# First projection in order of its contraction, modulation 512 columns wide, and the other vectors' sums a step ahead, in a DiT block with a mixture of experts

## The chip, the core and the metric

The kernel runs on one core of a Trainium2 chip. The metric is the device time of one execution in microseconds (us), less is better. TensorE (PE in the profile) multiplies matrices, VectorE (DVE), ScalarE (ACT) and GpSimd (POOL) work on rows, SyncE (SP) issues most loads. Each engine runs its own list of instructions in order and waits for the others by semaphores.

## What is computed

One transformer block on x, 512 tokens of 1024 channels, with 256 context tokens, all in float32. Cut to what matters:

```python
sh1, sc1, g1, sh2, sc2, g2 = split(silu(c) @ w_ada + b_ada)          # six vectors of 1024
csh1, csc1, *_             = split(silu(c_ctx) @ w_ada + b_ada)
hc = rms_norm(ctx, norm_mix) * (1 + csc1) + csh1
hx = rms_norm(x,   norm_mix) * (1 + sc1)  + sh1
q, zf_f, zf_b, i, g, gate_b, gate_c, v = split(hx @ w_in)            # eight sections of 512 columns
s_f, s_b = context_states(hc @ w_in[:, 512:2048])                    # zf_f, zf_b and i of ctx
o = gated_linear_attention(q, i, zf_f, zf_b, s_f, s_b)               # four heads, two directions
y = gate_b * conv3(gate_c * v)
x = x + g1 * (concat(rms_norm(o) * silu(g), y) @ w_out)
h2 = rms_norm(x, norm_ffn) * (1 + sc2) + sh2
x = x + g2 * expert_choice_ffn(h2)                                   # 16 experts, 64 tokens each
out = rms_norm(x, norm_final)
```

## The kernel before

All activations are kept transposed: channels on the 128 partitions, tokens in the free dimension. A weight of `w_in` or of the normalised input is split into a high and a low part in TensorE's fast float32 format (`whi`, `wlo`, L257 and L258; `h_hi`, `h_lo`, L292 to L294), and each product of the projections is made of three (L265, L266, L270 for x, L268, L269, L272 for ctx); `products` runs over the eight blocks `k` of the contraction for one block of 128 output columns at a time.

**Start.** SP loads ctx and the two halves of x (`xt`, L91), then weights in tiles of 1 MB (`stream`). `rms_rows` (L217, L220) normalises rows, `transpose_ctx` (L228) and `transpose_x` (L237) turn them on TensorE.

**Modulation.** The first two vectors, scale and shift, are worked out 256 columns at a time in eight units: `ada_unit` (L187) makes eight products, each with 32 columns of the array (`k % 4` chooses which 32), ACT copies the sum (L190), `ada_cols` transposes it twice (L197) and DVE adds the four groups (L198, L201). After each pair of units the two blocks `k` that it serves are modulated (L292 to L294), and section 1 (`zf_f`) uses them: its first half of 256 columns is made for two `k` at a time with four accumulators (`first`, two of x and two of ctx), its second half by `project_T` after all units.

**The other four vectors** (gate 1, shift 2, scale 2, gate 2) aren't made on TensorE: `ada_sum` loads 128x8x256 of `w_ada` and adds eight scaled tiles on DVE (L533, L535); one product with ones then adds over the partitions, as rows (`ada_r`, L543, with a DVE add L544) or as columns (`ada_c`, L550). `more_ada(j)` does one row sum and two column sums; it stands after the second half of section 1, the halves of section 2 and section 4. The four row sums of gate 2 (`g2b`) stand among the sections 6, 7, 5 in the head stage (`sections`).

**Then** come section 3 (`project_i`, L335) with the context states (`context_state`, L373 to L390), whose temporaries lie in the pool `p_c`; the router weight `wr`, loaded by POOL's queue (L613) behind `g2b` (L610) into the pool `rowb`, which takes the memory of the pools just released, and multiplied on DVE (L615); the head stage, which mixes attention of the four heads with the products of sections 0, 6, 7 and 5; the output projection, the router, and the experts (L897, L855, L954, L929), most of the time.

A scheduler sets the order on each engine: instructions are placed by the order of the program and by priority (`tc.high_priority`), each when its inputs can be there. In the code names have an index that the rows leave out.

Of the kernel before, what the change touches and what calls it, by code (L numbers as in the profile page):

```python
# [38 lines left out]
def dit_block(ctx, tc, x, c, ctx_in, c_ctx, w_ada, b_ada, norm_mix, norm_ffn, w_in, lb_logits,  # L39
# [164 lines left out]
    def ada_scale(ev, col0, dst, gain):  # L204

        ada_cols(ev, col0, dst)
        dve.tensor_scalar(dst, dst, 1.0, None, op0=ALU.add)
        dve.tensor_tensor(dst, dst, gain.unsqueeze(2).to_broadcast([P, 2, 2]), op=ALU.mult)
# [67 lines left out]
    first = None
    for j in range(4):
        ksl = slice(2 * j, 2 * j + 2)
        wsc, wsh = (stream(wa_r[:, :, at:at + 256], f"wa_{at}") for at in (D + 256 * j, 256 * j))
        with tc.high_priority(offset=PRIO if j else 0):  # L280
            ada_scale(ada_unit(D + 256 * j, wsc), D + 256 * j, a1[:, ksl], col("nmix", 2 * j, 2))
            ada_cols(ada_unit(256 * j, wsh), 256 * j, b1[:, ksl])
# [784 lines left out]
```

## Time and profile before

| | us |
|---|---|
| median of 3 runs | 1338.11 (1332.74 to 1338.48) |
| the profiled execution | 1336.76 |
| its span, first to last instruction | 1334.8 |
| TensorE busy | 1264.9 (95%) |
| DVE busy | 420.5 (32%) |
| ACT busy | 245.0 (18%) |
| POOL busy | 43.6 (3%) |
| data moved | 458.85 MB, mean 344 GB/s |

The profile is of one execution. PE is TensorE's products, PEld its weight loads, which overlap them. A float32 product leaves two records, one in the split format leaves one. PEclk is the granted TensorE clock as a share of full speed. In a row of the timeline the first number is the start, the second the duration, and the bracket at the end the idle time ahead of it and what ended that.

### The profile page before, as it was taken

How to read it: one execution, taken by the hardware profiler on the slowest of the kernel's cores; microseconds unless marked ns; L12 is line 12 of the kernel's file. 1: busy time of each engine (PE TensorE's matmuls, PEld its weight loads, DVE VectorE, ACT ScalarE, POOL GpSimd, SP SyncE). 2: the span in 40 equal slices, each digit the busy share in tenths (PEclk: the TensorE clock that was granted, in tenths of full speed). 3: DMA queues.
4: the chain of work that ended last, by engine and by line, in shares of the span. 5: the costliest groups of instructions: out<-in, count | busy, mean ns of one | idle time of the engine just before them, and what ended most of it. 6: DMA issues, size and time to landing. Idle time of an engine off the chain costs nothing.

```text
span 1334.8 us, 15459 instructions
## 1 busy us (share of the span) xinstructions
PE 1264.9 (95%) x6374; PEld 692.5 (52%) x6374; DVE 420.5 (32%) x969; ACT 245.0 (18%) x494; POOL 43.6 (3%) x51
## 2 busy tenths in 40 slices
PE   5999989998969999999999999999999999999996
PEld 3788978776844443444444344344434434443433
DVE  5776467986451112112101211211021121102114
ACT  5633444334211200010000001000000100000002
POOL 1000022140000000000000000000000000000000
PEclk9999989998979999999999999999999999999998
DMA  9868223316389989999999999999999999999996
GB/s 328 267 201 261 96 82 96 127 64 234 143 330 407 358 347 426 426 427 427 427 426 426 425 427 427 427 427 426 425 427 427 427 427 426 427 425 427 426 385 215
DMA packets 112082, 458.85 MB, mean 344 GB/s; under 512 B 7310, under 2 KB 56571, under 8 KB 64907
## 3 DMA queue, kind: packets, MB, share of 16 engines
q1 hardware_dynamic: 110832, 454.06, 84.6%
q0 software_dynamic: 992, 3.74, 0.8%
q8 instruction: 50, 0.82, 0.2%
q14 instruction: 22, 0.17, 0.0%
q10 hardware_dynamic: 186, 0.06, 0.0%
HBM read 455.73 MB, written 2.10 MB: 343 GB/s over the span
## 4 chain that ended last, share of the span: by engine, by line
PE 87%; DVE 7%; ACT 3%; DMA 2%; issue 1%; POOL 0%; DVEq 0%; ACTq 0%; POOLq 0%; SPq 0%
PE gu L897 37%; PE y L954 17%; PE pg L855 5%; PE po L929 3%; PE px L265 3%; PE px L266 3%; PE px L270 3%; PE ht L912 2%; PE y L1009 1%; PE wo L710 1%; PE wo L711 1%; PE wo L712 1%; DMA wd<-in_w_down 1%; PE pi L335 1%; PE pi L333 1%
## 5 line engine op out<-in xcount | busy, mean ns | idle before, releaser
L897 PE MATMUL gu<-wg,xs 128*64 128x512 f32 x1024 | 461.7, 599 | 0.7 <-ACT gs L907 0.7
L897 PE MATMUL gu<-wu,xs 128*64 128x512 f32 x1024 | 460.7, 599 | 0.0
L954 PE MATMUL y<-wd,hid 128*64 128x512 f32 x896 | 239.2, 598 | 0.0
L897 PEld LDWEIGHTS gu<-wg,xs 128*64 128x64 f32 x1024 | 128.7, 136 | 158.1 <-issue 154.3
L897 PEld LDWEIGHTS gu<-wu,xs 128*64 128x64 f32 x1024 | 128.7, 136 | 123.1 <-issue 122.5
L907 DVE COPY gs<-gu 128x512 f32<-128x512 f32 x32 | 22.0, 691 | 389.8 <-PE gu L897 389.8
L954 PEld LDWEIGHTS y<-wd,hid 128*64 128x64 f32 x896 | 82.2, 136 | 120.1 <-issue 113.8
L907 ACT COPY gs<-gu 128x512 f32<-128x512 f32 x32 | 18.7, 587 | 455.1 <-PE gu L897 455.1
L265 PE MATMUL px<-h_hi,whi 128*128 128x512 f32 x208 | 85.1, 409 | 0.0
L270 PE MATMUL px<-h_hi,wlo 128*128 128x512 f32 x208 | 84.0, 404 | 0.0
L855 PEld LDWEIGHTS pg<-ohr,x 128*128 128x128 f32 x512 | 62.4, 195 | 40.6 <-issue 38.9
L266 PE MATMUL px<-h_lo,whi 128*128 128x512 f32 x208 | 83.4, 401 | 0.0
L855 PE MATMUL pg<-ohr,x 128*128 128x128 f32 x512 | 71.8, 289 | 1.5 <-DVE ohr L847 1.5
L861 DVE TENSOR_SCALAR xs<-pg,a,b 128x128 f32<-128x128 f32 x32 | 13.1, 410 | 149.1 <-PE pg L855 149.1
L258 DVE TENSOR_TENSOR wlo<-wi,whi 128x1024 fp32r<-128x1024 f32 x32 | 42.3, 1326 | 34.4 <-ACT whi L257 34.3
L923 DVE SCALAR_TENSOR_TENSOR yt<-y,gate,g2b 128x512 f32<-128x512 f32 (+1 forms) x17 | 12.2, 719 | 128.8 <-PE y L954 108.6
L535 DVE SCALAR_TENSOR_TENSOR adas<-wa,cs,adas 128x256 f32<-128x256 f32 x112 | 51.5, 492 | 1.2
L858 ACT ACTIVATE xs<-pg,b,a 128x128 f32<-128x128 f32 x32 | 14.6, 457 | 199.7 <-PE pg L855 199.7
L929 PE MATMUL po<-yhl,g 128*128 128x512 f32 (+1 forms) x136 | 41.7, 418 | 7.5 <-ACT yhl L924 7.0
L265 PEld LDWEIGHTS px<-h_hi,whi 128*128 128x128 f32 x208 | 40.2, 193 | 8.4 <-issue 0.4
L966 DVE TENSOR_TENSOR acc<-acc,po 128x512 f32<-128x512 f32 x56 | 36.0, 684 | 26.8 <-PE po L929 26.8
L929 PEld LDWEIGHTS po<-yhl,g 128*128 128x128 f32 x136 | 22.4, 189 | 42.1 <-ACT yhl L924 14.3
(323 smaller groups left out, 1310.2 us busy)
## 6 DMA issues: line engine op xcount, KB each, us to landing
wg<-in_w_gate SPq DMA_DIRECT2D x128, 1024.0 KB, 17.4
wu<-in_w_up SPq DMA_DIRECT2D x128, 1024.0 KB, 18.1
wd<-in_w_down SPq DMA_DIRECT2D x124, 1024.0 KB, 19.5
wa<-in_w_ada SPq DMA_DIRECT2D x22, 1024.0 KB, 7.0
wi<-in_w_in SPq DMA_DIRECT2D x16, 1024.0 KB, 5.4
wo<-in_w_out SPq DMA_DIRECT2D x4, 1024.0 KB, 5.2
wd<-in_w_down SPq DMA_DIRECT2D x16, 256.0 KB, 5.9
xt<-in_x SPq DMA_DIRECT2D x2, 1024.0 KB, 7.7
```

The costliest lines, as they stand in the source:

```text
L258: dve.tensor_tensor(lo, v, hi.bitcast(F32), op=ALU.subtract)
L265: mm(px, hi[:, k], h_hi[:, k], start=f, stop=False)
L266: mm(px, hi[:, k], h_lo[:, k], start=False, stop=False)
L270: mm(px, lo[:, k], h_hi[:, k], start=False, stop=l)
L535: dve.scalar_tensor_tensor(acc, t[:, k * 256:(k + 1) * 256], cs[:, k, 0:1], acc, op0=ALU.mult, op1=ALU.add)
L855: mm(pg[:, :P], x1[:, tb, k * P:(k + 1) * P], ohr[:, tb], start=tb == 0, stop=tb == NT - 1)
L897: mm(gu[n][i * CAP:(i + 1) * CAP], xs[:, k, ssl], w[:, n * 512:(n + 1) * 512], start=k == 0, stop=k == KD - 1, skip_group_check=True)
L907: (act.copy if n % 2 else dve.tensor_copy)(to, fr)
L912: pe.transpose(pt[:, i * P:(i + 1) * P], gs[:, f * P:(f + 1) * P], ident)
L929: mm(po, g[:, tb * P:(tb + 1) * P], yhl[:, i, nsl], start=first and i == 0, stop=i == 1)
L954: mm(y[n][i * CAP:(i + 1) * CAP], hid[:, i, f], wd[i][:, s, n * 512:(n + 1) * 512], start=f == 0, stop=f == DFF // P - 1, skip_group_check ...
L966: dve.tensor_tensor(acc[tb][:, nsl], acc[tb][:, nsl], po, op=ALU.add)
```

## The change

Section 1 is made in the order of its contraction. `w_in` comes in two tiles of 512 rows by 512 columns; after the first pair of units, blocks 0 to 3 of x are multiplied with all 512 output columns (four accumulators of x, `first_x`), then blocks 0 to 3 of ctx (two banks, `first_c`), then blocks 4 to 7 of both. X is loaded, normalised and transposed first; ctx is loaded behind the first weights, and its rows are normalised and transposed behind the first products of x, through the bank "tp".

The modulation has four units of 512 columns instead of eight of 256. Their two tiles have rows of 2 KB instead of 1 KB. The transposes and the DVE reduction become four products with `sel`, a matrix of 128x2 that adds the groups.

The other vectors have eight sums of 512 columns instead of sixteen of 256, and the generator `others` makes the product of a sum one step after the sum: a step is one block of section 2, a half of section 4, or a half of section 3. Those of gate 2 lie there too, none in the head stage. `g2b` is loaded at the start. The gate's `kk` (L365 before) is issued after the table load that the projections are followed by. All else is as before.

```diff
-    for src, name in ((cx_r, "xt_c"), (x_r[:, 0:2], "xt_0"), (x_r[:, 2:4], "xt_1")):
+    for src, name in ((x_r[:, 0:2], "xt_0"), (x_r[:, 2:4], "xt_1"), (cx_r, "xt_c")):
         t = early.tile([P, 2048], F32, name=name)
-        sp.dma_start(out=t.rearrange("p (a b) -> p a b", a=2), in_=src)
+        if name != "xt_c":
+            sp.dma_start(out=t.rearrange("p (a b) -> p a b", a=2), in_=src)
         xt.append(t)
+    xt = xt[2:] + xt[:2]
...
+    def ada_loads(col0):
+        return [stream(wa_r[:, 4 * q:4 * q + 4, col0:col0 + 512], f"wa_{col0}_{q}")
+                for q in range(2)]
+
+    def ada_unit(col0, ts):
+        pa = bank("o", 1, f"ada_{col0}")
         for k in range(KD):
             g = k % 4
-            mm(pa[32 * g:32 * g + 32, :256], cs[:, k, :], t[:, k * 256:(k + 1) * 256],
+            mm(pa[32 * g:32 * g + 32], cs[:, k, :], ts[k // 4][:, g * 512:(g + 1) * 512],
                start=k < 4, stop=k >= 4, skip_group_check=True)
-        ev = early.tile([P, 256], F32, tag="adaev", name=f"ada_ev_{col0}", bufs=2)
-        act.copy(ev, pa[:, :256])
+        ev = early.tile([P, 512], F32, tag="adaev", name=f"ada_ev_{col0}", bufs=1)
+        act.copy(ev, pa)
         return ev
...
+    def ada_cols(ev, col0, dst, bias):
 
         pt = bank("tp", 1, f"ada_t_{col0}")
-        for b in range(2):
-            pe.transpose(pt[:, b * P:(b + 1) * P], ev[:, b * P:(b + 1) * P], ident)
-        dve.tensor_reduce(dst, pt[:, :256].rearrange("p (b g m) -> p b m g", b=2, g=4)[:, :, 0:2],
-                          op=ALU.add, axis=AX.X)
-        o = off["b_ada"] + col0 // P
-        dve.tensor_tensor(dst, dst, cols[:, o:o + 2].unsqueeze(2).to_broadcast([P, 2, 2]),
-                          op=ALU.add)
+        for b in range(4):
+            mm(pt[:, 2 * b:2 * b + 2], ev[:, b * P:(b + 1) * P], sel, start=b == 0, stop=b == 3,
+               skip_group_check=True)
+        dve.tensor_tensor(dst, pt[:, 0:8].rearrange("p (b m) -> p b m", b=4),
+                          bias.unsqueeze(2).to_broadcast([P, 4, 2]), op=ALU.add)
+
+    def ada_shift(ev, j, dst):
+        ada_cols(ev, 512 * j, dst, col("b_ada", 4 * j, 4))
+
+    def ada_scale(ev, j, dst, gain):
+
+        ada_cols(ev, D + 512 * j, dst, bias1[:, 4 * j:4 * j + 4])
...
-            pt = bank("mm", 4, f"pt_c_{k2}")
+            pt = bank("tp", 1, f"pt_c_{k2}")
...
+    first_x = [bank("mm", 4, f"px_f{i}") for i in range(4)]
+    first_c = [bank(tag, 1, f"pc_f_{tag}") for tag in ("sc", "kv")]
+    first_w = {}
...
+    def first_products(k, ctx_too):
+        hi, lo = (t[:, k % 2] for t in first_w[k // 2])
+        for i in range(4):
+            f, l, bs = k == 0, k == KD - 1, slice(i * P, (i + 1) * P)
+            if ctx_too:
+                pc = first_c[i // 2][:, (i % 2) * CTX:(i % 2 + 1) * CTX]
+                mm(pc, hi[:, bs], hc_hi[:, k], start=f and i % 2 == 0, stop=False,
+                   skip_group_check=True)
+                mm(pc, hi[:, bs], hc_lo[:, k], start=False, stop=False, skip_group_check=True)
+                mm(pc, lo[:, bs], hc_hi[:, k], start=False, stop=l, skip_group_check=True)
+            else:
+                mm(first_x[i], hi[:, bs], h_hi[:, k], start=f, stop=False)
+                mm(first_x[i], hi[:, bs], h_lo[:, k], start=False, stop=False)
+                mm(first_x[i], lo[:, bs], h_hi[:, k], start=False, stop=l)
+
+    def first_parts(n):
+        hi, lo = (p_h.tile([P, 2, 512], F32R, tag="whl", name=f"w{q}_1_{n}", bufs=6)
+                  for q in ("hi", "lo"))
+        v = raws[n // 2].rearrange("p (k n) -> p k n", k=4)[:, 2 * (n % 2):2 * (n % 2) + 2]
+        act.copy(hi, v)
+        dve.tensor_tensor(lo, v, hi.bitcast(F32), op=ALU.subtract)
+        first_w[n] = hi, lo
...
+    def modulation(j):
+        ksl = slice(4 * j, 4 * j + 4)
+        ada_scale(ada_unit(D + 512 * j, wsc[j]), j, a1[:, ksl], col("nmix", 4 * j, 4))
+        ada_shift(ada_unit(512 * j, wsh[j]), j, b1[:, ksl])
+
+    wsc, wsh = [ada_loads(D)], [ada_loads(0)]
+    first_raw = lambda i: stream(wi_r[:, 4 * i:4 * i + 4, 512:1024], f"wi_1_{i}")
+    raws = [first_raw(0)]
+    sp.dma_start(out=xt[0].rearrange("p (a b) -> p a b", a=2), in_=cx_r)
+    for i in range(2):
+        rms_rows(xt[1 + i], f"x{i}")
+    with tc.high_priority(offset=PRIO):
+        modulation(0)
+    transpose_x()
+    wsc.append(ada_loads(D + 512))
+    wsh.append(ada_loads(512))
+    raws.append(first_raw(1))
+    for j in range(2):
+        ks = range(4 * j, 4 * j + 4)
+        for n in (2 * j, 2 * j + 1):
+            first_parts(n)
+            for k in (2 * n, 2 * n + 1):
+                modulate(xnT, h_hi, h_lo, k, 0)
+        for k in ks:
+            first_products(k, False)
         if j == 0:
             rms_rows(xt[0], "c")
             transpose_ctx()
-            for i in range(2):
-                rms_rows(xt[1 + i], f"x{i}")
-            transpose_x()
-        for k in (2 * j, 2 * j + 1):
-            for src, hi, lo, m in ((xnT, h_hi, h_lo, 0), (cnT, hc_hi, hc_lo, 1)):
-                sca, sft = a1[:, k, m:m + 1], b1[:, k, m:m + 1]
-                act.activation(hi[:, k], src[:, k], AF.Identity, scale=sca, bias=sft)
-                dve.tensor_scalar(src[:, k], src[:, k], sca, sft, op0=ALU.mult, op1=ALU.add)
-                dve.tensor_tensor(lo[:, k], src[:, k], hi[:, k].bitcast(F32), op=ALU.subtract)
-        if first is None:
-            parts = split_w(1, 0)
-            first = [(bank("mm", 4, f"px_f{i}"), bank("mm", 4, f"pc_f{i}")) + parts[i]
-                     for i in range(2)]
-        for px, pc, hi, lo in first:
-            products(px, pc, hi, lo, (2 * j, 2 * j + 1))
+        for k in ks:
+            modulate(cnT, hc_hi, hc_lo, k, 1)
+            first_products(k, True)
+        if j == 0:
+            with tc.high_priority(offset=80):
+                modulation(1)
...
+        with tc.issue_after(tables.ins):
+            act.activation(kk, s, AF.Identity, scale=noml[:, i:i + 1], bias=oml[:, i:i + 1])
...
-        t = stream(wa_r[:, :, col0:col0 + 256], f"wa_{col0}")
-        acc = p_sig.tile([P, 256], F32, tag="adas", name=f"adas_{col0}", bufs=2)
-        dve.tensor_scalar(acc, t[:, :256], cs[:, 0, 0:1], None, op0=ALU.mult)
+        ts = ada_loads(col0)
+        acc = p_c.tile([P, 512], F32, tag="adas", name=f"adas_{col0}", bufs=2)
+        dve.tensor_scalar(acc, ts[0][:, :512], cs[:, 0, 0:1], None, op0=ALU.mult)
         for k in range(1, KD):
-            dve.scalar_tensor_tensor(acc, t[:, k * 256:(k + 1) * 256], cs[:, k, 0:1], acc,
-                                     op0=ALU.mult, op1=ALU.add)
+            dve.scalar_tensor_tensor(acc, ts[k // 4][:, (k % 4) * 512:(k % 4 + 1) * 512],
+                                     cs[:, k, 0:1], acc, op0=ALU.mult, op1=ALU.add)
...
+    g2b = const.tile([P, D], F32, name="g2b")
+    tc.keep_in_program_order(gp.dma_start(out=g2b, in_=bass.AP(
+        tensor=b_ada.tensor, offset=b_ada.offset + 5 * D, ap=[[0, P], [1, D]])))
...
+    def others():
+
+        last = None
+        for i, dst in ((3, b2), (4, a2), (2, g1b), (5, g2b)):
+            for j in range(2):
+                col0 = i * D + 512 * j
+                acc = ada_sum(col0)
+                if last:
+                    last()
+                if i == 3:
+                    last = lambda a=acc, c=col0, j=j: more_cols(a, c, b2[:, 4 * j:4 * j + 4])
+                elif i == 4:
+                    last = lambda a=acc, c=col0, j=j: more_scale(a, c, a2[:, 4 * j:4 * j + 4],
+                                                                 col("nffn", 4 * j, 4))
+                else:
+                    last = lambda a=acc, c=col0, j=j, d=dst: more_rows(a, c, d[:, 512 * j:512 * j + 512])
+                yield
+        last()
+        yield
+
+    more = others()
+    keep = keep_sig(0)
+    for i in range(4):
+        keep[0](i, first_x[i])
+        keep[1](i, first_c[i // 2][:, (i % 2) * CTX:(i % 2 + 1) * CTX])
+    for half in range(2):
+        for _ in project_T(2, half, *keep_sig(1)):
+            next(more)
     for half in range(2):
         run(project_T(4, half, keep_g))
-    more_ada(3)
-    tc.keep_in_program_order(act.preload_act_table_set("natural_log_exp_and_others"))
+        next(more)
...
+    tables = tc.keep_in_program_order(act.preload_act_table_set("natural_log_exp_and_others"))
     for half in range(2):
         project_i(half)
+        next(more)
         for h in (2 * half, 2 * half + 1):
             for d in range(2):
                 context_state(d, h)
+    run(more)
     p_c.release()
...
-    g2b = rowb.tile([P, D], F32, name="g2b")
-    gp.dma_start(out=g2b, in_=bass.AP(tensor=b_ada.tensor, offset=b_ada.offset + 5 * D,
-                                      ap=[[0, P], [1, D]]))
...
-                if i < 2:
-                    at = 256 * (2 * half + i)
-                    more_rows(5 * D + at, g2b[:, at:at + 256])
```

On TensorE, in section 1, behind the first products of x. `ada` are the units' sums (`spare` and `wa` their weights), `pt_c` transposes of ctx, `pc_f` products of ctx, `px_f` of x. Before:

```order
L270 MATMUL px_f_328<-h_hi,wlo_0_1_323 128x512
L187 MATMUL ada_504<-wa_500,cs 32x256 x8
L272 MATMUL pc_f_329<-hc_hi,wlo_0_1_323 128x256
L265 MATMUL px_f_326<-h_hi,whi_0_0_318 128x512
L268 MATMUL pc_f_327<-hc_hi,whi_0_0_318 128x256
```

Now:

```order
L311 MATMUL px_f_158<-h_hi,wlo_1_302 128x512
L193 MATMUL ada_457<-spare,cs 32x512
L239 MATMUL pt_c_373<-ident,xt_c 128x128
L193 MATMUL ada_457<-spare,cs 32x512
L239 MATMUL pt_c_373<-ident,xt_c 128x128
...
L304 MATMUL pc_f_sc<-hc_hi,whi_0_291 128x256
L304 MATMUL pc_f_kv<-hc_hi,whi_0_291 128x256
L306 MATMUL pc_f_sc<-hc_lo,whi_0_291 128x256
L307 MATMUL pc_f_sc<-hc_hi,wlo_0_292 128x256
L193 MATMUL ada_475<-wa_0_285,cs 32x512
L239 MATMUL pt_c_385<-ident,xt_c 128x128 x4
L193 MATMUL ada_475<-wa_0_285,cs 32x512 x3
L193 MATMUL ada_475<-wa_1_287,cs 32x512
L239 MATMUL pt_c_391<-ident,xt_c 128x128 x4
L193 MATMUL ada_475<-wa_1_287,cs 32x512 x3
```

A unit's eight products stood in one piece; now those of the first take turns with single transposes, eight times, and those of the second stand in three pieces.

On DVE, around the router weight's multiply (`wr`). `kk_c`, `pr_c`, `sigc` belong to context states, `wlo` to the splits of the next section. Before:

```order
L258 TENSOR_TENSOR wlo_1_0_1881<-wi_1_1878,whi_1_0_1880 128x1024
L373 SCALAR_TENSOR_TENSOR pr_c_1702<-ones,sigc_3_711 128x256
L379 TENSOR_TENSOR kk_c_1699<-kk_c_1699,sigc_3_711 128x256
L615 TENSOR_TENSOR wr_1761<-wr,a_585 128x128
L373 SCALAR_TENSOR_TENSOR pr_c_1719<-ones,sigc_3_1039 128x256
L377 TENSOR_TENSOR sigc_3_1039<-pr_c_1719,sigc_3_1039 128x256
```

Now:

```order
L598 TENSOR_TENSOR g2b<-g2b,ada_r_1556 128x512
L269 TENSOR_TENSOR wlo_1_0_1777<-wi_1_1774,whi_1_0_1776 128x1024
L428 SCALAR_TENSOR_TENSOR pr_c_1597<-ones,sigc_3_649 128x256
L598 TENSOR_TENSOR g2b<-g2b,ada_r_1629 128x512
L682 TENSOR_TENSOR wr_1657<-wr,a_633 128x128
L434 TENSOR_TENSOR kk_c_1594<-kk_c_1594,sigc_3_649 128x256
L428 SCALAR_TENSOR_TENSOR pr_c_1614<-ones,sigc_3_936 128x256
L432 TENSOR_TENSOR sigc_3_936<-pr_c_1614,sigc_3_936 128x256
```

The multiply stood behind the second to last context state's `kk`; now it stands ahead of it, and two adds of gate 2 stand close before.

On DVE in the head stage, at the norm of a head (`om`, `ou`, `or`, `on`). Before:

```order
L489 TENSOR_SCALAR om_2114<-os_2113 128x4
L426 TENSOR_TENSOR q2d_1755<-qT_1854,ex_2146 128x4x4x32
L490 TENSOR_TENSOR ou_2116<-or_2115 128x4
L533 TENSOR_SCALAR adas_2680<-wa_2678,cs 128x256
L491 TENSOR_TENSOR ou_2116<-ou_2116,om_2114 128x4
L535 SCALAR_TENSOR_TENSOR adas_2680<-wa_2678,cs,adas_2680 128x256
L492 TENSOR_SCALAR ou_2116<-ou_2116 128x4
L535 SCALAR_TENSOR_TENSOR adas_2680<-wa_2678,cs,adas_2680 128x256
```

Now:

```order
L544 TENSOR_SCALAR om_2010<-os_2009 128x4
L473 TENSOR_TENSOR kk_2030<-ki_2045,dte_2037 128x512
L545 TENSOR_TENSOR ou_2012<-or_2011 128x4
L546 TENSOR_TENSOR ou_2012<-ou_2012,om_2010 128x4
L547 TENSOR_SCALAR ou_2012<-ou_2012 128x4
L548 TENSOR_TENSOR or_2011<-or_2011,ou_2012 128x4
```

The sums of gate 2 (`adas`) stood between the steps of the norm; none is left there.

## Rows read from the trace of the kernel before

**Rows 1.** The page, chain that ended last, by engine.

```profile
PE 87%; DVE 7%; ACT 3%; DMA 2%; issue 1%; POOL 0%; DVEq 0%; ACTq 0%; POOLq 0%; SPq 0%
```

**Rows 2.** Busy time by stretch; columns as in the first line here.

```profile
core 0: us, PE busy (x) PEld busy (x) DVE busy (x) ACT busy (x) POOL busy (x), PEclk, DMA share, GB/s
0.00:26.50 26.50, 12.01 (x85) 8.76 (x85) 12.72 (x52) 14.05 (x26) 3.98 (x13) 1.00 0.98 323
...
71.40:131.70 60.30, 60.30 (x327) 51.90 (x325) 44.50 (x102) 20.13 (x28) 0.00 (x0) 1.00 0.72 226
...
170.90:206.00 35.10, 31.12 (x135) 25.51 (x134) 21.99 (x43) 14.29 (x30) 12.23 (x12) 0.85 0.38 117
206.00:311.00 105.00, 101.24 (x744) 83.81 (x742) 87.79 (x162) 40.31 (x93) 24.58 (x21) 0.98 0.28 90
...
390.50:1295.00 904.50, 890.81 (x3978) 387.59 (x3978) 141.65 (x322) 76.30 (x155) 0.54 (x1) 1.00 1.00 417
```

**Rows 3.** Timeline of PE, 12 to 33 us.

```profile
24.01 1.97 PE L237 MATMUL pt_x<-ident,xt 128*128 128x128 f32 x16 [0.17 <-ACT xnT L240]
26.56 0.49 PE L265 MATMUL px_f<-h_hi,whi 128*128 128x512 f32 x1 [0.58 <-ACT whi L257]
...
31.78 1.07 PE L187 MATMUL ada<-spare,cs 128*32 128x256 f32 x16
```

**Rows 4.** Timeline of DVE, then of ACT, 12 to 30 us.

```profile
15.50 1.42 DVE L220 TENSOR_SCALAR xt<-xt,r1r 128x1024 f32<-128x1024 f32 x2
...
21.18 0.75 DVE L220 TENSOR_SCALAR xt<-xt,r1r 128x1024 f32<-128x1024 f32 x1
...
24.75 0.81 ACT L292 ACTIVATE h_hi<-xnT,b,a 128x512 fp32r<-128x512 f32 x1 [0.31 <-DVE b L201]
25.47 1.03 ACT L257 CAST whi<-wi 128x1024 fp32r<-128x1024 f32 x1
```

**Rows 5.** Timeline of PE, 60 to 74 us.

```profile
61.94 0.39 PE L265 MATMUL px<-h_hi,whi 128*128 128x512 f32 x1
62.17 0.40 PE L266 MATMUL px<-h_lo,whi 128*128 128x512 f32 x1
62.40 0.28 PE L268 MATMUL pc<-hc_hi,whi 128*128 128x256 f32 x1
62.52 0.27 PE L269 MATMUL pc<-hc_lo,whi 128*128 128x256 f32 x1
...
71.41 0.59 PE L543 MATMUL ada_r<-adas,ones 128*128 128x256 f32 x2
71.84 0.50 PE L550 MATMUL ada_c<-ones,adas 128*128 128x2 f32 x4
72.21 0.48 PE L265 MATMUL px<-h_hi,whi 128*128 128x512 f32 x1
```

**Rows 6.** Timeline of all engines, 168 to 184 us.

```profile
170.88 0.55 POOL L610 DMA_DIRECT2D g2b<-in_b_ada  x1 [150.85 <-PE pt_c L382]
171.42 0.92 POOL L613 DMA_DIRECT2D wr<-in_w_router  x1
...
178.78 0.29 DVE L615 TENSOR_TENSOR wr<-wr,a 128x128 f32<-128x128 f32 x1 [4.04 <-DMA wr<-in_w_router]
...
181.19 0.41 PE L382 MATMUL pt_c<-ident,kk_c 128*128 128x128 f32 x2 [3.98 <-DVE kk_c L379]
```

**Rows 7.** Busy time and clock, two stretches after idle time; columns as in rows 2.

```profile
182.80:193.10 10.30, 10.30 (x36) 8.82 (x35) 7.53 (x17) 5.60 (x11) 5.36 (x5) 0.53 0.33 104
...
244.20:247.70 3.50, 3.50 (x10) 2.73 (x10) 3.50 (x9) 0.00 (x0) 0.00 (x0) 0.58 0.02 5
```

**Rows 8.** Waits of PE, 206 to 311 us: total, times, longest.

```profile
PE kv L456 <- ACT kT L443: 2.6, 2, 2.1
```

**Rows 9.** Groups of DVE, 206 to 311 us: busy, mean ns, idle before.

```profile
L535 DVE SCALAR_TENSOR_TENSOR adas<-wa,cs,adas 128x256 f32<-128x256 f32 x14 | 8.0, 572 | 0.1
...
L544 DVE TENSOR_TENSOR g2b<-g2b,ada_r 128x256 f32<-128x256 f32 x4 | 1.6, 412 | 0.0
```

More of the change, by code (lines that the diff above doesn't have):

```diff
@@ L204, in ada_scale @@
[L204 to L208, printed above, removed]
+        ev = early.tile([P, 512], F32, tag="adaev", name=f"ada_ev_{col0}", bufs=1)
+        act.copy(ev, pa)
+        return ev
+    sel = const.tile([P, 2], F32, name="sel")
+    dve.tensor_reduce(sel, ident.rearrange("p (g m) -> p m g", g=4)[:, 0:2], op=ALU.add, axis=AX.X)
@@ new lines, in dit_block @@
+    bias1 = const.tile([P, 8], F32, name="bias1")
+    dve.tensor_scalar(bias1, col("b_ada", 8, 8), 1.0, None, op0=ALU.add)
+    def ada_cols(ev, col0, dst, bias):
+        pt = bank("tp", 1, f"ada_t_{col0}")
+        for b in range(4):
[3 more added lines that the diff above has]
+                          bias.unsqueeze(2).to_broadcast([P, 4, 2]), op=ALU.add)
@@ L211, in dit_block @@
+    def ada_shift(ev, j, dst):
+        ada_cols(ev, 512 * j, dst, col("b_ada", 4 * j, 4))
+    def ada_scale(ev, j, dst, gain):
+        ada_cols(ev, D + 512 * j, dst, bias1[:, 4 * j:4 * j + 4])
+        dve.tensor_tensor(dst, dst, gain.unsqueeze(2).to_broadcast([P, 4, 2]), op=ALU.mult)
     xnT = early.tile([P, KD, SEQ], F32, tag="xnT", name="xnT")
@@ L275, in dit_block @@
     b1 = const.tile([P, KD, 2], F32, name="b1")
[L276 to L282, printed above, removed]
+    first_x = [bank("mm", 4, f"px_f{i}") for i in range(4)]
@@ new lines, in dit_block, with modulate @@
+    first_c = [bank(tag, 1, f"pc_f_{tag}") for tag in ("sc", "kv")]
+    first_w = {}
+    def modulate(src, hi, lo, k, m):
+        sca, sft = a1[:, k, m:m + 1], b1[:, k, m:m + 1]
+        act.activation(hi[:, k], src[:, k], AF.Identity, scale=sca, bias=sft)
+        dve.tensor_scalar(src[:, k], src[:, k], sca, sft, op0=ALU.mult, op1=ALU.add)
+        dve.tensor_tensor(lo[:, k], src[:, k], hi[:, k].bitcast(F32), op=ALU.subtract)
+    def first_products(k, ctx_too):
[12 more added lines that the diff above has]
+                mm(first_x[i], lo[:, bs], h_hi[:, k], start=False, stop=l)
@@ L364, in gates @@
         kk = pool.tile([P, w], F32, tag="kk", name=f"kk_{nm}", bufs=2)
-        act.activation(kk, s, AF.Identity, scale=noml[:, i:i + 1], bias=oml[:, i:i + 1])
+        with tc.issue_after(tables.ins):
+            act.activation(kk, s, AF.Identity, scale=noml[:, i:i + 1], bias=oml[:, i:i + 1])
         act.activation(s, s, AF.Ln, scale=oml[:, i:i + 1], bias=lb[:, i:i + 1])
@@ L510, in keep_gc @@
     def keep_gc(i, px):
-        cv[i] = p_sig.tile([P, SEQ], F32, tag="cv", name=f"cv_{i}", bufs=2)
+        cv[i] = p_in.tile([P, SEQ], F32, tag="cv", name=f"cv_{i}", bufs=2)
         act.copy(cv[i], px)
@@ L537, in ada_sum, with more_rows @@
-        return acc
-    def more_rows(col0, dst):
-        acc = ada_sum(col0)
+            dve.scalar_tensor_tensor(acc, ts[k // 4][:, (k % 4) * 512:(k % 4 + 1) * 512],
+                                     cs[:, k, 0:1], acc, op0=ALU.mult, op1=ALU.add)
+        return acc
+    def more_rows(acc, col0, dst):
         pg = bank("mm", 4, f"ada_r_{col0}")
-        mm(pg[:, :256], ones[:, :P], acc, start=True, stop=True)
-        dve.tensor_tensor(dst, dst, pg[:, :256], op=ALU.add)
-    def more_cols(col0, dst):
-        acc = ada_sum(col0)
+        mm(pg, ones[:, :P], acc, start=True, stop=True)
+        dve.tensor_tensor(dst, dst, pg, op=ALU.add)
@@ L548, in more_cols @@
+    def more_cols(acc, col0, dst):
         pg = bank("tp", 1, f"ada_c_{col0}")
-        for b in range(2):
+        for b in range(4):
             mm(pg[:, 2 * b:2 * b + 2], acc[:, b * P:(b + 1) * P], ones[:, 0:2], start=b == 0,
-               stop=b == 1, skip_group_check=True)
+               stop=b == 3, skip_group_check=True)
         o = off["b_ada"] + col0 // P
-        dve.tensor_tensor(dst, pg[:, 0:4].rearrange("p (b m) -> p b m", b=2),
-                          cols[:, o:o + 2].unsqueeze(2).to_broadcast([P, 2, 2]), op=ALU.add)
@@ L556, in more_scale @@
-    def more_scale(col0, dst, gain):
-        more_cols(col0, dst)
+        dve.tensor_tensor(dst, pg[:, 0:8].rearrange("p (b m) -> p b m", b=4),
+                          cols[:, o:o + 4].unsqueeze(2).to_broadcast([P, 4, 2]), op=ALU.add)
+    def more_scale(acc, col0, dst, gain):
+        more_cols(acc, col0, dst)
         dve.tensor_scalar(dst, dst, 1.0, None, op0=ALU.add)
-        dve.tensor_tensor(dst, dst, gain.unsqueeze(2).to_broadcast([P, 2, 2]), op=ALU.mult)
+        dve.tensor_tensor(dst, dst, gain.unsqueeze(2).to_broadcast([P, 4, 2]), op=ALU.mult)
@@ L572, in dit_block @@
-    for d in range(2):
-        for half in range(2):
-            keep = keep_sig(d)
-            if d == half == 0:
-                for i, (px, pc, hi, lo) in enumerate(first):
-                    keep[0](i, px)
-                    keep[1](i, pc[:, :CTX])
-            else:
-                run(project_T(1 + d, half, *keep))
-                more_ada(2 * d + half - 1)
+    def others():
[16 more added lines that the diff above has]
+        yield
```

8 lines of the change are left out of this document (removed).

## Prediction, written before the changed kernel was run

> **What bounds the kernel now.** I read the chain of waits first: TensorE holds 87% of it, DVE 7%, DMA 2% [rows 1]. Whatever shortens TensorE's own list of work, or its idle time, moves the end. Then the stages, by a table of stretches: in the longest one, the experts, TensorE is busy 890.81 of 904.50 us [rows 2]. The change touches nothing there, and the loads of that part start when buffers of the head stage come free, so it shifts as a whole by what the first 311 us gain or lose. Those early stages differ. In the projections of 71 to 132 us TensorE never rests, while DVE works 44.50 of 60.30 us: there work moved onto DVE is free, work on TensorE is paid in full. Around the router weight, 171 to 206 us, and in the head stage, 206 to 311 us, TensorE idles 35.10 - 31.12 = 4.0 and 105.00 - 101.24 = 3.8 us [rows 2]: only there can a wait be won.
>
> The sum is made against the profiled execution, 1336.76 us, 1.35 below the median of 1338.11 and inside the runs' 1332.74 to 1338.48. A measurement can tell some 0.5%, 6.7 us, from no change.
>
> **Start of the products.** Before, the last tile of x is normalised at 21.18 + 0.75 = 21.9 us, behind ctx and the first x tile (ready at 15.50 + 1.42 = 16.9) [rows 4], and the first product starts at 26.56 [rows 3]. Now x comes first, so its last tile should be ready when its first one was, at 16.9. After it stand, in the order listed: 8 transposes (half of the 1.97 for 16 [rows 3], 1.0); the second half of the scale unit; 16 more transposes (2.0); its sums by `sel`; the shift unit; its eviction and sums; two modulations and one split.
>
> What a unit costs: 8 products of 256 columns on 32 array columns each take 1.07 us together [rows 3]. One float32 product of 256 columns costs 71.84 - 71.41 = 0.43 us [rows 5], so four column groups do run at once (two rounds, 0.86) and 0.21 goes into the change of shape. At 512 columns two rounds are 1.72, a packed unit 1.93, half of one 1.0. The sums by `sel` are 4 products with two columns; two such products, in four records, took 72.21 - 71.84 = 0.37 [rows 5], so 0.74. Eviction of 512 columns: no more than the 0.81 of the activation of that shape [rows 4]. So 16.9 + 1.0 + 1.0 + 2.0 + 0.74 + 1.93 + 0.8 + 0.74 + 2 x 0.81 + 1.03 [rows 4] = 27.8, and one wait like the 0.58 ahead of the first product now [rows 3]: **28.4**. What x won, the wider units take back.
>
> **The first section.** It ends at 71.41 now [rows 5]. After: 28.4, plus 96 products of x at 62.17 - 61.94 = 0.23 us (22.1) and 96 of ctx at 62.52 - 62.40 = 0.12 (11.5) [rows 5], plus three things now behind the first product: 16 ctx transposes (2.0; they ran while TensorE had nothing else to do), two sums by `sel` (1.5), and the other two units. These are the doubtful ones. The order puts products of the first of them singly between ctx transposes of full width, and cuts the second into three pieces. Then the groups can't run together: a product alone is 2 x 0.43 = 0.86 and, by the 0.21 found above, 1.07 with its change of shape; 8 x 1.07 + 3 x 1.07 = 11.8. No row shows such an alternation. [...] The end is 28.4 + 22.1 + 11.5 + 2.0 + 1.5 + 11.8 = 77.3: **+5.9**.
>
> [...] The row of the unit shows 0.21 us beyond two rounds of streams [rows 3]. [...]
>
> Ctx is loaded eighth now. Eight loads of 1.05 MB at the 323 GB/s of the first 26.5 us [rows 2] are in by 26 us, and its normalising has to begin by about 33, six us ahead of its transposes; I count no wait.
>
> **Sections two to four.** Before, these held four row sums (0.43) and eight column sums (0.37) [rows 5]: 4.7 us. Now four column sums of twice the width (0.74) and one row sum (0.86): 3.8. **-0.9.** DVE's part, now with 512 columns in an operation, hides in the 16 us that DVE has free there [rows 2]; the sum being a step ahead, TensorE doesn't wait for it. Table loads that go are on ACT and hide behind products: nothing. The third 512-wide row sum and its DVE add go into the projection of i: +0.86, with 0.37 of column sums less, and some 1 us for context states that now have fewer products between them: **+1.5** (0 to 2.5).
>
> **The router weight.** POOL issues g2b at 170.88 and the router weight behind it at 171.42; DVE's multiply waits 4.04 us for it, the context state behind that on DVE waits too, and TensorE idles 3.98 until 181.19 [rows 6]. The idle engine then runs 10.30 us at a clock of 0.53 [rows 7], a loss of some (1 - 0.53) x 10.30 = 4.8. Together 8.8. Now g2b is loaded at the start, const; the router weight still waits for the same memory to come free and its flight remains (178.78 less 171.42 is 7.4 us [rows 6], which it had to share). On DVE its multiply stands ahead of one more context state, so less work is left to cover the flight; against that, two row sums of 0.86 (+1.7) fill TensorE. I take 2.0 us of idle time and half of the slow clock, 2.4: 1.7 + 2.0 + 2.4 = 6.1 instead of 8.8: **-2.7**. Bounds: nothing but the 1.7 is left (-7.1), or the wait stays and 1.7 is added (+1.7).
>
> **The head stage.** Four row sums leave it: 4 x 0.43 = 1.7 on TensorE. On DVE 8.0 us of multiplies and 1.6 of adds go [rows 9], and they stand among the steps whose results TensorE and ACT wait for. Its idle 3.8 us there is for keys from ACT, 2.6 of it [rows 8], that come behind DVE's steps, and the clock after it, 0.58 for 3.50 us, costs 1.5 [rows 7]. I give the change 80% of 5.3: 4.3. **-6.0**, bounds -1.7 and -7.0.
>
> Sum: +5.9 - 0.9 + 1.5 - 2.7 - 6.0 = -2.2, from 1336.76: **1334.6 us**.
>
> **The rivals.** *The alternation costs nothing.* The column groups overlap across the transposes; for it, that they do so inside a unit [rows 3]. 11.8 becomes 3.9: 1334.6 - 7.9 = 1326.7. Against it: TensorE takes its list in order, and each transpose needs all columns. Chance 0.12.
>
> *The router weight comes early.* With the queue to itself it lands before it is asked for; stall and slow clock vanish. 4.4 better, 1330.2. For it, that it was issued only 0.54 us behind the other load [rows 6] and landed with it; against it, the longer queue on DVE. Chance 0.17.
>
> [...] Chance 0.11.
>
> *DVE doesn't hold the head stage.* The wait for keys is ACT's own, as the row names ACT [rows 8]; then only the 1.7 of TensorE is won, 4.3 worse: 1338.9. Chance 0.09.
>
> **How the numbers follow.** The forecast has 0.51. Its own terms (1.5 on the projection of i, 4 on the router weight, 2 on the head stage) give 1330 to 1339. The range, 1325 to 1345, takes in the first, second and fourth rivals with their edges and stops just short of the third's price; outside lie the third rival and a few edges, under 0.2. Faster than 1331.4: the first rival, two thirds of the second, a tenth of the forecast: 0.12 + 0.11 + 0.05 = 0.28. Slower than 1344.8: the third, and 0.02 where the upper ends of several terms meet: 0.13. The rest 0.59.
>
> **What would show it.** In the trace after: first product near 28.4; narrow products and transposes in turn near 39 to 49 at about 1.07 a pair; the first section's end near 77.3; from there to the projection of i one us less than before; around the router weight an idle time of about 2 us in place of 3.98 and a clock above 0.53; the head stage about 99 us instead of 105, with less than 1 us waited for keys; and the experts' 904.5 unchanged. The prediction is wrong if the units take 4 us, if the clock drops there, or if the experts' stage itself changes in length.

## The result, and the profile after

The change is slower: 1346.07 us (1345.24 to 1347.96, four runs) against 1335.55 (1332.74 to 1338.48), a ratio of 1.0095 with an interval of 1.0071 to 1.0118. The forecast was 1334.6, range 1325 to 1345. The profiled execution took 1345.24 us, its span is 1343.5, 8.7 longer than before. The loads in the page's 40 slices tell something at once, before:

```profile
GB/s 328 267 201 261 96 82 96 127 64 234 143 330 407 358 347 426 426 427 427 427 426 426 425 427 427 427 427 426 425 427 427 427 427 426 427 425 427 426 385 215
```

and now:

```profile
GB/s 359 196 198 254 204 104 68 63 64 286 137 327 394 356 363 422 421 421 420 421 421 421 421 421 420 421 421 421 421 421 421 420 422 421 421 421 421 421 371 229
```

From slice 16 to 38 it was 425 to 427 GB/s, and now it is 420 to 422.

The stretches of the changed kernel, cut where its stages end (columns as in [rows 2]):

```profile
core 0: us, PE busy (x) PEld busy (x) DVE busy (x) ACT busy (x) POOL busy (x), PEclk, DMA share, GB/s
0.00:28.50 28.50, 12.51 (x82) 7.32 (x82) 11.79 (x47) 11.88 (x21) 2.64 (x11) 0.99 0.94 354
28.50:42.40 13.90, 13.90 (x48) 10.97 (x48) 7.32 (x15) 4.50 (x7) 1.88 (x3) 0.78 0.90 336
42.40:57.00 14.60, 14.60 (x54) 3.99 (x53) 3.17 (x8) 5.34 (x10) 0.00 (x0) 1.00 0.27 75
57.00:80.90 23.90, 23.86 (x160) 21.60 (x158) 19.78 (x35) 13.13 (x20) 0.00 (x0) 1.00 0.55 184
80.90:140.10 59.20, 59.20 (x324) 51.13 (x323) 37.24 (x55) 14.25 (x23) 0.00 (x0) 1.00 0.76 254
...
176.00:213.00 37.00, 34.07 (x212) 27.78 (x211) 23.61 (x40) 18.79 (x35) 12.37 (x11) 1.00 0.29 85
213.00:311.00 98.00, 95.05 (x695) 79.36 (x693) 80.21 (x142) 40.16 (x91) 24.64 (x21) 1.00 0.23 77
```

The clock is 1.00 around the router weight (176 to 213), where it was 0.53 for 10.30 us [rows 7], and in the alternating stretch (42.4 to 57); it is low (0.78) where before it wasn't, behind 28.5 us. TensorE's timeline shows the first section:

```profile
24.70 1.05 PE L208 MATMUL ada_t<-sel,ada_ev 128*128 128x2 f32 x8 [0.76 <-ACT ada_ev L196]
28.50 0.79 PE L309 MATMUL px_f<-h_hi,whi 128*128 128x512 f32 x1 [2.74 <-ACT whi L317]
29.09 0.63 PE L310 MATMUL px_f<-h_lo,whi 128*128 128x512 f32 x1
...
42.46 1.04 PE L193 MATMUL ada<-spare,cs 128*32 128x512 f32 x2
43.43 0.33 PE L239 MATMUL pt_c<-ident,xt_c 128*128 128x128 f32 x1
43.69 1.04 PE L193 MATMUL ada<-spare,cs 128*32 128x512 f32 x2
...
52.17 0.36 PE L304 MATMUL pc_f_sc<-hc_hi,whi 128*128 128x256 f32 x1
...
54.40 1.07 PE L193 MATMUL ada<-wa,cs 128*32 128x512 f32 x8
...
80.89 0.39 PE L276 MATMUL px<-h_hi,whi 128*128 128x512 f32 x1
```

The first product starts at 28.50 (26.56 before [rows 3]). A product of a unit in turn with a transpose takes 43.69 - 42.46 = 1.23 us a pair; four products in one piece take 1.07 together (eight records, two to a product). Section 2 starts at 80.89.

Around the router weight, all engines (answers to [rows 6]):

```profile
179.79 0.92 POOL L680 DMA_DIRECT2D wr<-in_w_router  x1 [144.19 <-PE pi L389]
...
180.14 1.02 PE L597 MATMUL ada_r<-adas,ones 128*128 128x512 f32 x2
...
185.92 0.29 DVE L682 TENSOR_TENSOR wr<-wr,a 128x128 f32<-128x128 f32 x1 [2.75 <-DMA wr<-in_w_router]
...
186.69 0.41 PE L437 MATMUL pt_c<-ident,kk_c 128*128 128x128 f32 x2 [2.93 <-DVE kk_c L434]
```

TensorE idles 2.93 us instead of 3.98. In the head stage the waits of TensorE are now these (190 to 311 us); the wait for `kT`, 2.6 us [rows 8], is gone:

```profile
PE sc L502 <- POOL q2d L486: 0.5, 1, 0.5
PE pt_o L557 <- DVE on L550: 0.3, 1, 0.3
PE o L531 <- DVE both L528: 0.2, 1, 0.2
```

So the first section ends later than before (80.89 us for 71.41), and the stages behind it win that back: the output projection's first product starts at 315.11 us, where before it started at 317.07, 2.0 us ahead. What makes the change slower lies behind that, in the experts. The gathers of each second expert (`pg`) mark the pace there. Before:

```profile
930.90 1.38 PE L855 MATMUL pg<-ohr,x 128*128 128x128 f32 x10
...
1046.61 1.38 PE L855 MATMUL pg<-ohr,x 128*128 128x128 f32 x10
...
1162.31 1.38 PE L855 MATMUL pg<-ohr,x 128*128 128x128 f32 x10
```

After:

```profile
929.59 1.38 PE L919 MATMUL pg<-ohr,x 128*128 128x128 f32 x10
...
1050.18 1.38 PE L919 MATMUL pg<-ohr,x 128*128 128x128 f32 x10
...
1169.45 1.38 PE L919 MATMUL pg<-ohr,x 128*128 128x128 f32 x10
```

At 930 us the changed kernel is still 1.3 us ahead. Up to there a pair of experts takes 115.71 us in both. Then it takes 120.59 and 119.27 in the changed one. By the last product the 1.3 us ahead have become 8.7 behind (1332.5 us for 1323.8).

A pair of experts loads 48 tiles of 1.05 MB, 50.3 MB; in 115.71 us that is 435 GB/s, more than the loads give in either kernel. So the loads fall behind TensorE all the time, and TensorE lives on the buffers that were filled ahead. At 427 GB/s a pair is short by 115.71 x (1 - 427/435) = 2.1 us, at 421 by 3.7 (estimates from these rows). The spacings fit: at 427 the reserve lasts to the end, at 421 to a point behind 930 us, and after that a pair takes 119.27 us, which is 50.3 MB at 422 GB/s, the rate of the loads. What has to be explained is the 421.

### The profile page after: what moved, and what is told of

Read it like the earlier page. It is cut to its first block, busy times and chain, and to the rows that moved or that the text cites. A ratio compares the mean times of both kernels' runs of the same rounds, so it can differ in the third digit from the quotient of the medians.

```text
span 1343.5 us, 15244 instructions
## 1 busy us (share of the span) xinstructions
PE 1276.5 (95%) x6318; PEld 690.5 (51%) x6318; DVE 409.5 (30%) x877; ACT 237.3 (18%) x484; POOL 44.3 (3%) x51
## 4 chain that ended last, share of the span: by engine, by line
PE 91%; DVE 4%; DMA 2%; ACT 2%; issue 1%; POOL 0%; DVEq 0%; SPq 0%; POOLq 0%; ACTq 0%
PE gu L961 38%; PE y L1018 17%; PE pg L919 5%; PE px L276 3%; PE px L277 3%; PE px L281 3%; PE po L993 3%; PE ht L976 2%; PE y L1073 1%; PE wo L774 1%; PE ada L193 1%; PE wo L775 1%; PE wo L776 1%; DMA wd<-in_w_down 1%; PE pi L389 1%
## 5 line engine op out<-in xcount | busy, mean ns | idle before, releaser
L961 PE MATMUL gu<-wg,xs 128*64 128x512 f32 x1024 | 462.4, 599 | 0.7 <-ACT gs L971 0.7
L276 PE MATMUL px<-h_hi,whi 128*128 128x512 f32 x192 | 76.8, 400 | 0.0
L281 PE MATMUL px<-h_hi,wlo 128*128 128x512 f32 x192 | 75.3, 392 | 0.0
L277 PE MATMUL px<-h_lo,whi 128*128 128x512 f32 x192 | 74.9, 390 | 0.0
L269 DVE TENSOR_TENSOR wlo<-wi,whi 128x1024 fp32r<-128x1024 f32 x28 | 37.4, 1335 | 27.3 <-ACT whi L268 27.2
L590 DVE SCALAR_TENSOR_TENSOR adas<-wa,cs,adas 128x512 f32<-128x512 f32 x56 | 41.4, 748 | 1.4 <-DMA wa<-in_w_ada 0.4
L976 PE MATMUL ht<-ident,gs 128*128 128x128 f32 x256 | 34.9, 279 | 6.9 <-DVE hid L980 6.9
```

The source lines that it names most:

```text
L269: dve.tensor_tensor(lo, v, hi.bitcast(F32), op=ALU.subtract)
L276: mm(px, hi[:, k], h_hi[:, k], start=f, stop=False)
L277: mm(px, hi[:, k], h_lo[:, k], start=False, stop=False)
L281: mm(px, lo[:, k], h_hi[:, k], start=False, stop=l)
L590: dve.scalar_tensor_tensor(acc, ts[k // 4][:, (k % 4) * 512:(k % 4 + 1) * 512], cs[:, k, 0:1], acc, op0=ALU.mult, op1=ALU.add)
L961: mm(gu[n][i * CAP:(i + 1) * CAP], xs[:, k, ssl], w[:, n * 512:(n + 1) * 512], start=k == 0, stop=k == KD - 1, skip_group_check=True)
```

## The experiments

**Theory A:** the address of the weight buffers. In the built program the twelve weight buffers of `ring_b` start at byte 80896 of a partition before, a multiple of 512; in the changed one at 80960, 64 further. `g2b` left `rowb` for `const`, both ahead of `ring_b`, which cancels; `sel` and `bias1`, of 8 and 32 bytes, take the 64. The four buffers of `ring_a` lie 352 and 416 bytes past a multiple of 512. **Theory B:** the order of the work, or the state in which the stage is entered.

The first six kernels (a_b0 to a_ra0_b64 below) differ from their base in unused tiles alone; every engine's list of instructions is the same as in the base. The unused tile in `rowb` moves what is allocated behind it on the same side by the same bytes: the twelve buffers, and some tiles that hold no streamed weights (the router's, the parts of `w_out`, the rows that the experts gather).

**a_b0**, changed kernel:

```diff
     rowb = tc.alloc_tile_pool(name="rowb", bufs=1, side="left")
+    rowb.tile([P, 112], F32, name="pad")
```

> The changed kernel with an unused tile of 448 bytes per partition in the pool rowb, which lies ahead of the twelve weight buffers of the experts (ring_b); every engine's list of instructions stays as it is, and the buffers start at a multiple of 512 bytes again, as before the change, instead of 64 bytes past one. Theory A, the address of the buffers sets the rate of the loads: loads of the experts' stage back at 427 GB/s instead of 421, pairs of experts 115.7 us apart to the end instead of 119.3 in the last third, and the time is what the first 315 us say, 2 us under the kernel before: about 1334. Theory B, the order of the work or the state in which the stage is entered slows the loads: 421 GB/s and 1346 as the change.

Measured: 1334.85 us, ratio to before 1.0002 (0.9988 to 1.0016; each ratio is against runs of the kernel before that were taken beside it, with medians of 1332.45 to 1334.62). Its stretches in the experts:

```profile
550.00:950.00 400.00, 394.64 (x1767) 172.69 (x1764) 61.04 (x136) 31.26 (x66) 0.00 (x0) 1.00 1.01 427
950.00:1250.00 300.00, 295.63 (x1310) 127.19 (x1309) 48.86 (x104) 23.11 (x48) 0.54 (x1) 1.00 1.01 426
```

and those of the change:

```profile
550.00:950.00 400.00, 394.65 (x1767) 172.75 (x1764) 61.07 (x136) 31.31 (x66) 0.00 (x0) 1.00 1.01 421
950.00:1250.00 300.00, 295.63 (x1268) 126.39 (x1265) 48.19 (x102) 22.56 (x47) 0.54 (x1) 1.00 1.01 421
```

The loss shows in a count only: from 950 on, 1268 records of products against 1310 in 300 us, while TensorE's busy time is 295.63 in both. The page of the change says why busy time can't show it:

```profile
L961 PE MATMUL gu<-wg,xs 128*64 128x512 f32 x1024 | 462.4, 599 | 0.7 <-ACT gs L971 0.7
```

1024 records of 599 ns would be 613 us one behind another, and are busy for 462.4: a record reaches over the start of the next, so a start that comes a little later leaves no idle time. That these starts wait for loads is inferred from the spacing and the rate, since no row names such a wait.

**b_b64**, the kernel before with the same line and 16 in place of 112.

> The kernel before with an unused tile of 64 bytes per partition in rowb, so that the twelve buffers lie at the very addresses that they have in the changed kernel, 64 bytes past a multiple of 512; nothing else differs. Theory A: 421 GB/s in the experts' stage, the pairs of experts 119.3 us apart from about 950 us on, and some 10.7 us more than the kernel before: about 1346. Theory B: as the kernel before, 427 GB/s, 1335.5.

Measured: 1343.99 us, ratio 1.0074 (1.0049 to 1.0100).

```profile
550.00:950.00 400.00, 394.65 (x1765) 172.90 (x1765) 61.80 (x140) 31.75 (x67) 0.00 (x0) 1.00 1.01 421
950.00:1250.00 300.00, 295.63 (x1274) 127.41 (x1272) 48.13 (x102) 22.67 (x47) 0.54 (x1) 1.00 1.01 421
```

64 bytes that nobody uses make the old kernel's loads as slow in the experts as the changed one's, 421 GB/s in both. Theory A holds, B falls. Of the 10.7 us that I expected 8.4 came, by the medians.

**a_b256** (48 in place of 112), **a_b128** (16, changed kernel), and two that also move the four older buffers to a multiple of 512 by an unused tile of 96 bytes in `const`: **a_all0** (with 88 in `rowb`, all sixteen aligned) and **a_ra0_b64** (104, only those four).

> The changed kernel with an unused tile of 192 bytes in rowb: the buffers start 256 bytes past a multiple of 512. Theory A with a boundary of 256 bytes: 427 GB/s and about 1334, as with 448 bytes. Theory A with a boundary of 512 bytes: 421 GB/s and 1346. Theory B: 1346.

> The changed kernel with unused tiles that put the four older buffers (ring_a, 416 bytes past a multiple of 512 in the change, 352 before) on a multiple of 512 too, and the twelve as well. Theory A: with twelve of sixteen buffers aligned 427, with none 421, so all sixteen give about 429 GB/s; the time is no better than about 1333, since at 427 TensorE sets the pace of the experts. Theory B: 421 GB/s, 1346.

> The changed kernel with the four older buffers on a multiple of 512 and the twelve still 64 bytes past one: one look at the rate of the loads. If each misaligned buffer costs alike, four aligned of sixteen give 422 to 423 GB/s; if what counts is that any load in flight is misaligned, or only the twelve, 421; with the time 1344 to 1346.

> The changed kernel with an unused tile of 64 bytes in rowb: the twelve buffers start 128 bytes past a multiple of 512. If the boundary that counts is 256 bytes, as 256 past one (427 GB/s) and 64 past one (421) would have it: 421 GB/s and 1344 to 1347. If it is 128 bytes: 427 and 1335.

Measured, with the loads' rate from 550 to 950 us:

| kernel | ring_b past 512 | ring_a past 512 | GB/s | us |
|---|---|---|---|---|
| before | 0 | 352 | 427 | 1335.55 |
| the change | 64 | 416 | 421 | 1346.07 |
| a_b0 | 0 | 416 | 427 | 1334.85 |
| b_b64 | 64 | 352 | 421 | 1343.99 |
| a_b256 | 256 | 416 | 427 | 1335.28 |
| a_all0 | 0 | 0 | 427 | 1336.79 |
| a_b128 | 128 | 416 | 421 | 1346.45 (two runs) |
| a_ra0_b64 | 64 | 0 | 423 | 1344.47 (one run) |

0 and 256 give the full rate, 64 and 128 don't: by these four offsets what counts is a multiple of 256 bytes. Four aligned buffers of sixteen bring 2 GB/s of the 6, in the one run of a_ra0_b64, as expected if each costs alike. The other tiles of `rowb` and behind it lie 64 bytes past a boundary there as in the change, which speaks for the buffers of the loads and against those tiles. All sixteen bring no more than twelve: the 429 that I expected isn't there, so that each costs alike holds for the four and not to the end; why 427 is the end stays open.

Off the boundary is the side that the loads write, and the loss is the same at 64 bytes and at 128, 1.4% (421 for 427 GB/s). By what mechanism an offset costs it no run shows.

**The parts of the change, with aligned buffers.** **b_others** takes the start, the eight units and the first section of the kernel before, and all else of the change:

```diff
-    for i in range(4):
-        keep[0](i, first_x[i])
...
+    for i, (px, pc, hi, lo) in enumerate(first):
+        keep[0](i, px)
+        keep[1](i, pc[:, :CTX])
+    run(project_T(1, 1, *keep))
```

> The start, the modulation in eight units and the first section as before the change; the other vectors' sums, g2b and the rest as in the change; the twelve buffers on a multiple of 512 bytes. Theory C, the new first section loses what the other parts gain: its products start near 26.5 us instead of 28.5, it ends some 9.5 us earlier than in the change (71.4 against 80.9), and all of that stays: 1334.9 - 9.5 = about 1325.5, faster than both kernels. Theory D, what the later parts win comes of the later start (weights have arrived, waits shrink) or is lost to waits: 1330 to 1335.

Measured: 1328.17 us, ratio 0.9954 (0.9939 to 0.9969), 6.7 under a_b0. In its trace section 2 starts at 71.49 us and the output projection at 308.22, 9.4 and 7.0 ahead of a_b0. The result lies between the two theories and nearer to C: the new first section is a loss and the rest a gain, and of the 9.4 us some 7 arrive; the rest goes on the way to the output projection, as theory D has it.

**a_pack**, from a_b0:

```diff
-            with tc.high_priority(offset=80):
+            with tc.high_priority(offset=PRIO):
                 modulation(1)
```

> The changed kernel with aligned buffers, and the second pair of units put ahead of the ctx transposes by a higher priority: their products stand in four pieces of four, and the transposes in pieces of four or eight, instead of one by one. Theory of the alternation: two units and 16 transposes took 13.8 us; now 4 x 1.07 + 4 x 0.65 = 6.9, so 1334.9 - 6.9 = 1328. Rival: the units' weights haven't landed where they now stand, TensorE waits for them ahead of work that was ready: 1333 to 1336.

Measured: 1327.58 us, ratio 0.9955 (0.9939 to 0.9971), 7.3 under a_b0. The units' products now stand in pieces of four (eight records), three of them among products of x:

```profile
35.59 1.06 PE L193 MATMUL ada<-spare,cs 128*32 128x512 f32 x8
39.08 1.07 PE L193 MATMUL ada<-wa,cs 128*32 128x512 f32 x8
42.57 1.07 PE L193 MATMUL ada<-wa,cs 128*32 128x512 f32 x8
44.84 0.60 PE L239 MATMUL pt_c<-ident,xt_c 128*128 128x128 f32 x4
```

They don't wait for their weights. From the first product to section 2 it takes 45.2 us (27.64 to 72.80) where the change takes 52.4 (28.50 to 80.89), with 6.8 us of slow clock (0.5) in both: the alternation's price is some 7 us.

**a_g2head**: the sums of gate 2 back into `sections`, from a kernel like a_b256; `others` ends with g1b.

```diff
                 yield from project_T(sec, half, keep)
+                if i < 2:
...
+                    mm(pg[:, :256], ones[:, :P], acc, start=True, stop=True)
```

> The changed kernel with aligned buffers (256 past 512), and the sums of gate 2 put back into the head stage, four of 256 columns between the sections 6, 7 and 5 as before the change. Theory of the prediction, these sums on DVE hold TensorE up in the head stage: 6 us more than with aligned buffers alone, 1341, with a wait for keys (kT) of over 1 us back and a stretch of slow clock after it. Rival, they lie beside TensorE's work: only a longer wait around the router weight, within 2 us of 1335.

Measured: 1340.75 us, ratio 1.0044 (1.0029 to 1.0058), 5.5 over a_b256. Its head stage has the old wait back, to the tenth, and the stretch of slow clock (3.4 us) too:

```profile
PE kv L511 <- ACT kT L498: 2.6, 2, 2.1
```

From the first product of the scores (`sc`) to the output projection it takes 110.7 us, in a_b256 104.0 and in the kernel before 110.7. Ahead of that, from the projection of i on, a_g2head takes 71.8 us and a_b256 72.5: that the sums are no longer there wins next to nothing.

**Beyond both kernels.** **a_wr** is a_pack with `wr` in `const`, loaded at the start behind `g2b`; **a_split** is a_pack with the first cast of weights put ahead of the modulation on ACT; **a_both** has both.

```diff
-    wr = rowb.tile([P, KD, E], F32, name="wr")
+    wr = const.tile([P, KD, E], F32, name="wr")
...
-            first_parts(n)
-            for k in (2 * n, 2 * n + 1):
-                modulate(xnT, h_hi, h_lo, k, 0)
+            cast = first_parts(n)
+            with tc.issue_after(cast.ins):
+                for k in (2 * n, 2 * n + 1):
+                    modulate(xnT, h_hi, h_lo, k, 0)
```

> a_pack with the router weight loaded at the start, into the pool const, behind g1b and g2b on POOL's queue. Theory of the stall: what is left of it is the flight of this load, asked for at 179.8 and multiplied at 185.9, with the context states behind it on DVE. Without it TensorE's 2.9 us of idle time goes, and the slow clock after it, which a_pack had for 3.4 us (1.7 lost): 1327.6 - 2.9 to 4.6 = 1323 to 1325. Rival, the context states' own chain over ACT and DVE takes the place of the wait: 1327.

> a_pack with the first split of weights put ahead of the modulation on ACT, so that ACT casts them while it waits for the shift's sums. Theory: the first product waits 2.74 us behind two modulations and a cast, 2.9 us after the sums; with the cast done before it starts 1 to 1.7 us earlier, and if it is this idle time that sets the clock to 0.5 for 6.8 us, a shorter one keeps it at 1.0 and 3.4 more come: 1322.5 to 1326.6. Rival: the clock falls as before, since the engine had little work all the while before, and the weights land too late for the cast: 1327.6.

> a_pack with both edits, that of a_wr and that of a_split. If they are independent, the sum of their gains: between 1318 and 1324. If not, as the better of the two.

Measured: a_wr 1324.78 us, 0.9922 (0.9904 to 0.9940); a_split 1327.23, 0.9944 (0.9925 to 0.9962); a_both 1324.07, 0.9918 (0.9898 to 0.9938). In a_wr TensorE no longer waits there at all, and 2.8 us are won by the medians: the flight of the router weight was what was left of the stall. a_split wins nothing that can be told, and its rival is right about the clock, which falls for 6.8 us as in the change, not about the weights: the cast is done in time (from 24.66 us for 1.05, ahead of the first modulation at 26.11). TensorE starts earlier and stops again:

```profile
26.97 1.29 PE L309 MATMUL px_f<-h_hi,whi 128*128 128x512 f32 x4 [1.11 <-ACT h_hi L294]
28.86 0.79 PE L310 MATMUL px_f<-h_lo,whi 128*128 128x512 f32 x1 [0.59 <-DVE h_lo L296]
```

The gain of a_both over a_wr is not to be told from nothing. a_wr and a_both are the fastest; by their intervals b_others, a_pack and a_split are faster than the kernel before too, all by less than 1%.

## Why the prediction was wrong, and where it was right

| step | forecast | measured |
|---|---|---|
| first product starts | 28.4 | 28.50 |
| end of the first section, against 71.41 | +5.9 | 80.89: +9.5 |
| of it: two units and 16 transposes | 13.8 | 9.7 (first unit, 8 transposes) + 4.1 (second, 8) = 13.8 |
| sections two to four | -0.9 | 59.23 for 60.26: -1.0 |
| projection of i to the first scores | +1.5 - 2.7 = -1.2 | 70.96 for 74.66: -3.7 |
| head stage, to the output projection | -6.0 | 104.03 for 110.74: -6.7 |
| experts, with what lies ahead and behind | 0 | +10.7 |

The first scores, before and now, start at:

```profile
206.33 0.54 PE L447 MATMUL sc<-q2d,ki 128*32 128x128 f32 x12
211.08 0.54 PE L502 MATMUL sc<-q2d,ki 128*32 128x128 f32 x12
```

The step that failed is the one that I gave least thought: "The change touches nothing there", and that the experts shift as a whole. It was put at nothing and measured +10.7 us. The instructions there are indeed the same. Their buffers aren't where they were: 64 bytes further, which takes the loads from 427 to 421 GB/s, as a_b0 and b_b64 show. The rows said what margin there was: DMA share 1.00 at 417 GB/s beside a busy TensorE [rows 2]. I read it as TensorE's stage; loads and products were in fact so close that 1.4% on the loads used up the reserve.

The third rival, that the clock falls in the alternating stretch, stood at 1346.4, the price that the range stops short of and almost the time that came: the forecast with the 11.8 us of the units doubled. No run shows that doubling, nor that narrow products lower the clock: in its place, 42.4 to 57 us, the clock is 1.00. Its number is no support for it. The first rival falls with the 13.8 us. A product in turn with a transpose took 1.23 us a pair: a product alone at 0.86 and a transpose at 0.12 (1.97 for 16 [rows 3]) leave 0.25 over. That the 0.21 in the forecast is the price of a change of shape was my estimate; no run tells what the 0.25 is spent on.

The first section's other 3.6 us are a term that I put at nothing: the clock at 0.5 for 6.8 us from the first product on, which costs 3.4. The idle time ahead of it was in my sum: between the last sums by `sel` and the first product it has two modulations, a split and a wait of 0.58, 3.2 us in all, and 2.74 were measured. That the clock could fall behind it, as the rows show behind other idle times (0.53 and 0.58 [rows 7]), I left out.

The head stage was right in mechanism and size: 6.7 for 6.0, and a_g2head loses 5.5 again. The router weight came out at 2.9 us of idle time where I took 2.0, without slow clock where I took 2.4 lost. That its stage won 3.7 us is luck: behind the wait the clock was slow for 10.2 us in the profiled execution before and not at all in that of the change. In b_b64, whose instructions are those of before, the stretch took 71.2 us with 3.4 at slow clock; in the five kernels with the instructions of the change it took 70.98 to 75.40 with 0 to 6.8. The means, 72.9 for the two and 72.5 for the change and the five, give -0.5 where I had -1.2.

So the forecast's terms hold for the work of the first section, for sections two to four and for the head stage. The clock behind the first product and the experts were missed, and the gain around the router weight is not to be told from nothing. With the buffers back on their boundary a_b0 comes at 1334.85 us for the forecast 1334.6, which is luck too: against the kernel before it is no difference (1.0002) where I forecast 2.2 us less, and in its trace, as in the change's, no slow clock behind the router weight makes up for the first section's miss.

## What to carry to other kernels

Look at the addresses of large load buffers after every change that adds a small tile to a pool ahead of them, and keep them on a multiple of 256 bytes (here 427 GB/s at 0 and 256 bytes past, 421 at 64 and 128); a stage "untouched" by a diff may have moved in memory. Where a stage runs with its loads at full share (here 1.00), work out its margin (bytes per step over the step's time, against the rate) before saying that it is bound by an engine, and watch counts and spacings, since the records of TensorE's products overlapped here (1024 of 599 ns busy for 462.4 us), and TensorE was busy for 295.63 us of 300 with 1268 records as with 1310. Keep products on narrow column groups in one piece, and don't let a scheduler thread full-width ones between them: here four in one piece took 1.07 us, one in turn with a transpose 1.23, and a_pack came out 7.3 us under a_b0.
